# Four input projections of a hybrid mixer as seven products of quarters each

## The chip, the cores and the metric

The kernel runs on one core of a Trainium2 chip. The metric is the device time of one execution in microseconds (us). The engines of the core are TensorE (PE in the profile, its weight loads PEld), VectorE (DVE), ScalarE (ACT), GpSimd (POOL) and SyncE (SP), which issues nearly all DMAs. Each engine takes its own instructions strictly in order and waits at an instruction until the semaphores that it needs have been raised.

## What is computed

One decoder layer on 512 tokens of width 1024, in float32: a SwiGLU feed-forward part, a token mixer and a second feed-forward part, each between two RMS norms.

```python
x = x + 0.5 * rms_norm(swiglu_ffn(rms_norm(x, norm_pre[0]), ffn1_w_in, ffn1_w_out), norm_post[0])
x = x + rms_norm(token_mixer(rms_norm(x, norm_pre[1]), w_mix_in, ...), norm_post[1])
x = x + 0.5 * rms_norm(swiglu_ffn(rms_norm(x, norm_pre[2]), ffn2_w_in, ffn2_w_out), norm_post[2])

def token_mixer(h, w_in, ...):
    hq, hf, hi, hgate, mq, mk, mv, mo, mig, mfg = split_cols(h @ w_in, SPLIT_SIZES)
    # HGRN2 heads from hq, hf, hi, times silu(hgate); mLSTM heads from conv(mq, mk), mv and gates,
    # times sigmoid(mo); both normed, joined, and multiplied by w_out
```

The products `hi`, `hgate`, `mv` and `mo` are each 512 tokens by 1024 inputs by 512 columns.

## The kernel before

A float32 product is made of three TensorE products: each operand is split into a high part (rounded to the type fp32r) and a low part (the rest), and hi·hi, hi·lo and lo·hi are added in PSUM. The normed x of the mixer is held transposed and split in `xq`, four tiles: two halves of the tokens by two halves of the width. Weights come by DMA from SP's queue in tiles of 128 x 1024 values (512 KB) into a ring `raw`; `split` makes the high part on ScalarE (L273) and the low part on VectorE (L275) in one of four slots `w`. `feed` keeps up to four split tiles ahead of TensorE. Where sums of weight tiles are wanted (the feed-forward parts already use seven products for eight), `split` adds them on GpSimd or VectorE (L289).

The mixer writes out its order by hand. Projections are generators in a queue `jobs`; `fill(n)` takes n steps from it, and a step is some 0.7 us of matmuls. The main line calls `fill` between its own small steps, so that TensorE has matmuls while the other engines work on the recurrence. The order of jobs is `hq` (4), `conv` (4), `rows` (the gates), `hi`, `mv`, later `hg` and `mo`. A scheduling layer then orders each engine's instructions by its own model.

The main line is: `forget_gates` (the rest of the `hf` products, sigmoid, log, scans into `G`), on GpSimd meanwhile `gate_weights` and `masks`; then `hgrn_levels` for head pair 0 and for head pair 1. A level takes two differences of `G` on VectorE (L1284, L1285), two exponentials on ScalarE (`qe` L1286, `ke` L1287), a product (L1291), sixteen small matmuls (L1302) and a masked copy (L1306), with `FILL[0]` = 6 or `FILL[1]` = 5 steps of projections between. Then `hgrn_states`, `mlstm_scores`, `mlstm_values`, `hgrn_values` and the output product `mix_out0`, `mix_out1`.

The four projections go through `job_t`: per projection four weight tiles, and for each tile four blocks of 128 tokens by two blocks of 128 inputs by three parts, 96 matmuls of 512 columns in all (L179, L180, L181). ScalarE copies the result of each token block out of PSUM. The residual x stays in the tile `xs` in SBUF from the first feed-forward part until `post1` adds to it (L493).

Of the kernel before, what the change touches and what calls it, by code (L numbers as in the profile page):

```python
# [8 lines left out]
F32 = mybir.dt.float32  # L9
F32R = mybir.dt.float32r  # L10
AF = mybir.ActivationFunctionType
# [3 lines left out]
P = 128  # L15
# [11 lines left out]
QUARTER = 256  # L27
FILL = (6, 5, 2, 2)
NH = 4
# [9 lines left out]


HEAD = 3
FILLED = 4
# [51 lines left out]
FREE2 = (3, 2, 0, 1)  # L94
LIES = {"any": (0, -16, -80, 48), "mix": (-16, 0, -80, 48), "out": (-80, 48, 0, -16)}

# [19 lines left out]
class Layer:  # L116
    def __init__(self, ctx, tc, aps):
        self.tc, self.nc = tc, tc.nc
        self.__dict__.update(aps)
        nc = self.nc  # L120
        pool = lambda name, **kw: ctx.enter_context(tc.tile_pool(name=name, bufs=1, **kw))
        self.cp, self.wp, self.sp, self.psp = pool("cp"), pool("wp"), pool("sp"), pool("psp", space=PSUM)
        self.uid, self.hold = 0, ()
        self.wt, self.free, self.slot = None, deque(), {}

        self.ident = self.cp.tile([P, P], F32, name="ident")
        make_identity(nc, self.ident)
        self.nhalf = self.cp.tile([P, 8], F32, name="nhalf")
        nc.gpsimd.memset(self.nhalf, -0.5)
        self.xs = self.cp.tile([P, NT, D], F32, name="xs")  # L130
# [7 lines left out]
        self.prm = self.cp.tile([P, 36], F32, name="prm")  # L138

    def nm(self, s):  # L140
# [76 lines left out]
    def load_due(self, n):  # L217
        lds = self.due.pop(n, ())
        for ld in lds:
            pool = self.wp if ld.ring == "raw" else self.hpool  # L220
# [29 lines left out]
    def split(self):  # L250
# [5 lines left out]
        if it.dst:  # L256
            w = it.dst()
        else:
            if self.wt is None:
                self.wt = self.wp.tile([P, 2 * D * WBUF + FRONT + PAD], F32R, name="w")  # L260
            if not self.slot and it.key[0] != "mix":
                self.free = deque(FREE2 if it.key[0] == "f2" else FREE)
            n, o = self.lie("out" if it.key[1] == "out" else "mix" if it.key[0] == "mix" and b == 512 else "any")
# [20 lines left out]
        with self.behind(*self.hold):  # L284
            for out, other in it.adds:
                o, c = self.raw[out], self.raw[other]

                late = out[1] >= (HEAD if out[0] == "f1" else 1)
                (nc.vector if late else nc.gpsimd).tensor_tensor(o, o, c, op=ALU.add)  # L289
# [742 lines left out]

    def job_t(self, name, then):

        acc = [self.ps() for _ in range(NT)]
        for k2 in range(ND // 2):
            w = self.pull()
            for i in range(NT):
                for kk in range(2):
                    self.t_mm(acc[i], w, 2 * k2 + kk, kk, i)  # L1040
                    if kk == 0:
                        yield
                if i == NT - 1:
                    self.drop(w)
                if k2 == ND // 2 - 1:
                    then(i, acc[i])
                    if i == NT - 1:
                        self.got.add(name)
                yield

    def mix_items(self):
# [16 lines left out]

        f(HF), f(HQ), f(MQ), t(HI), t(MV), t(HG), t(MO)
        for h in range(2):  # L1070
# [131 lines left out]
    def forget_gates(self, mb):  # L1202
# [14 lines left out]
        for p, f in enumerate(fs):  # L1217
            for a in range(2):
# [3 lines left out]
                )  # L1222
            kk = mb.tile([P, 2, T], F32, tag="kk", bufs=2, name=self.nm("kk"))
            nc.vector.tensor_scalar(kk, f, -1.0, 1.0, op0=ALU.mult, op1=ALU.add)
# [220 lines left out]
    def conv(self, n, ps):  # L1445

        nc = self.nc
        x = self.st("cx")
        nc.scalar.copy(x, ps)
        tap = lambda j: self.prm[:, 4 * j + n : 4 * j + n + 1]  # L1450
        y = self.qk[:, n, :]
# [29 lines left out]
    def mlstm_scores(self, mc):  # L1481
# [14 lines left out]
        nc.scalar.activation(w, w, AF.Exp)  # L1496
        self.qdm = mc.tile([P, 2, 3 * P], F32, name="qdm")
        self.kw = mc.tile([P, 2, 3, P], F32, name="kw")
# [120 lines left out]
    def mixer(self):  # L1619
        nc, tc = self.nc, self.tc  # L1620
        self.got, self.jobs = set(), deque()
        with tc.tile_pool(name="ma", bufs=1) as ma:
# [6 lines left out]
            self.S = self.kdt.rearrange("p h (c v) -> p h c v", v=P)  # L1629
            self.eend = ma.tile([P, 16], F32, name="eend")  # L1630
            with tc.tile_pool(name="mb", bufs=1) as mb:
                self.mb = mb
                kes = [mb.tile([P, 2, T], F32, name=f"ke{n}") for n in range(2)]
                self.q = [mb.tile([P, 2, T], F32, tag="q", bufs=2, name=f"q{p}") for p in range(2)]
# [6 lines left out]
                self.jobs.append(self.job_t("hi", lambda i, ps: nc.scalar.copy(self.vh[:, i].rearrange("p h v -> p (h v)"), ps)))  # L1641
                self.jobs.append(
                    self.job_t("mv", lambda i, ps: nc.scalar.copy(self.vm[:, i, :, :P], ps.rearrange("p (h v) -> p h v", h=NH)))
                )

# [5 lines left out]
                with tc.issue_after(self.pow.ins):  # L1651
                    nc.gpsimd.memset(self.sT, 0.0)
                    self.masks(ma, mb)
                    nc.gpsimd.memset(self.vm[:, :, :, P : P + 1], 1.0)
                self.until("hq3")
                for n in range(NH):
                    nc.scalar.activation(self.q[n // 2][:, n % 2], qps[n], AF.Silu)
                self.hgrn_levels(0, kes, FILL[0])
                self.until("rows")
                nc.scalar.activation(self.qk, self.qk, AF.Silu)  # L1660
                self.hgrn_levels(1, kes, FILL[1], self.gate_rows(ma))
            with tc.tile_pool(name="mc", bufs=1) as mc:
                self.y = mc.tile([P, NT, D], F32, name="y")
                self.jobs.append(self.job_t("hg", lambda i, ps: nc.scalar.activation(self.y[:, i, :W], ps, AF.Silu)))
                self.until("hi")
                self.hgrn_states()
                self.mlstm_scores(mc)
                self.jobs.append(self.job_t("mo", self.gate_mo))
                self.chunks(self.mlstm_values, FILL[2])
# [7 lines left out]
    def gate_mo(self, i, ps):  # L1677
        nc = self.nc
        g = self.st("mo")
        nc.scalar.activation(g, ps, AF.Sigmoid)  # L1680
        y = self.y[:, i, W:]
        nc.vector.tensor_tensor(y, y, g, op=ALU.mult)
# [129 lines left out]
```

## Time and profile before

| | |
|---|---|
| median of 3 runs | 940.24 us (940.08 to 941.1) |
| span of the profiled execution | 938.5 us, 1.74 below the median |
| TensorE busy | 930.2 us, 7471 matmuls |
| VectorE busy | 772.4 us |
| ScalarE busy | 511.9 us |
| GpSimd busy | 107.4 us |

The profile is of one execution. The only time known for the profiled execution itself is its span, from the first instruction to the last; the runs were timed from outside and are other executions. A row of a timeline has the start and the duration in us, the engine, the line of the kernel, the operation and its tiles; what stands in brackets is idle time of the engine just before, and what ended it. A row of a group has the number of instructions, then busy time in us and the mean of one in ns. Durations of neighbours on one engine overlap a little (by about 0.08 us on VectorE).

### The profile page before, as it was taken

To read this page: it belongs to the slowest core of one execution; us is meant where nothing else is said; L and a number is where in the kernel's file an instruction comes from. 1 tells how busy PE (TensorE), PEld (TensorE's weight loads), DVE (VectorE), ACT (ScalarE), POOL (GpSimd) and SP (SyncE) were. 2 spreads that over 40 slices of the span, in tenths; PEclk is the share of its full clock that TensorE was granted. 3 is DMA by queue.
4 is the path that set the end of the run, shared out by engine and by line. 5 is a ranking of instruction groups with operands and counts; after the bars stand their busy time and mean duration, and the time that the engine had idled before them with its cause. 6 is when DMAs were issued, how large, how long until landed. Compare 5 with 4: busy or idle time off the path is not lost.

```text
span 938.5 us, 18056 instructions
## 1 busy us (share of the span) xinstructions
PE 930.2 (99%) x7471; PEld 895.9 (95%) x7471; DVE 772.4 (82%) x1044; ACT 511.9 (55%) x735; POOL 107.4 (11%) x172
## 2 busy tenths in 40 slices
PE   9999999999999999999999999999999999999997
PEld 7999999999999999998887888899999999999997
DVE  6899988889988876698846564799899989998884
ACT  7645555557456467956622444495454545655541
POOL 3530000000001045200001210314000000000101
PEclk9999999999999999999999999999999999999999
DMA  9252433332352024321312124352354434323212
GB/s 319 87 157 91 126 123 113 93 111 72 118 170 90 24 84 124 111 68 45 91 45 68 45 76 139 123 173 65 124 158 135 135 115 156 113 87 121 87 45 90
DMA packets 86956, 101.35 MB, mean 108 GB/s; under 512 B 4277, under 2 KB 66777, under 8 KB 86874
## 3 DMA queue, kind: packets, MB, share of 16 engines
q1 hardware_dynamic: 86586, 99.68, 34.0%
q8 instruction: 58, 0.95, 0.4%
q10 hardware_dynamic: 288, 0.52, 0.2%
q14 instruction: 24, 0.20, 0.1%
HBM read 98.10 MB, written 2.10 MB: 107 GB/s over the span
## 4 chain that ended last, share of the span: by engine, by line
PE 63%; ACT 1%; issue 0%; DVE 0%; DVEq 0%; POOLq 0%; POOL 0%; ACTq 0%
PE ps L603 22%; PE ps L893 7%; PE ps L533 6%; PE ps L901 5%; PE ps L179 5%; PE ps L181 5%; PE ps L180 5%; PE ps L1302 2%; PE ps L543 1%; PE ps L348 1%; PE ps L1476 0%; PE ps L1387 0%; PE ps L1583 0%; PE ps L1556 0%; PE ps L1342 0%; PE ps L1580 0%
## 5 line engine op out<-in xcount | busy, mean ns | idle before, releaser
L273 ACT CAST w<-raw 128x1024 fp32r<-128x1024 f32 (+1 forms) x238 | 244.6, 1035 | 230.3 <-PE ps L603 93.5
L275 DVE TENSOR_TENSOR w<-raw,w 128x1024 fp32r<-128x1024 f32 (+1 forms) x238 | 290.9, 1228 | 36.3 <-ACT w L273 35.8
L603 PE MATMUL ps<-xq,w 128*128 128x256 f32 x2016 | 237.1, 277 | 0.0
L603 PEld LDWEIGHTS ps<-xq,w 128*128 128x128 f32 x2016 | 232.9, 188 | 0.0
L603 PE MATMUL ps<-sq,w 128*128 128x256 f32 x1512 | 177.9, 276 | 0.3
L603 PEld LDWEIGHTS ps<-sq,w 128*128 128x128 f32 x1512 | 174.3, 188 | 0.9 <-ACT ps L654 0.9
L893 PE MATMUL ps<-w,hs 128*128 128x256 f32 x960 | 113.0, 276 | 0.0
L893 PEld LDWEIGHTS ps<-w,hs 128*128 128x128 f32 x960 | 110.7, 188 | 0.0
L289 DVE TENSOR_TENSOR raw<-raw,raw 128x1024 f32<-128x1024 f32 x72 | 89.8, 1251 | 6.1 <-DMA raw<-in_ffn_w_in_dram 4.5
L179 PE MATMUL ps<-w,xq 128*128 128x512 f32 x192 | 78.7, 411 | 0.1
L180 PE MATMUL ps<-w,xq 128*128 128x512 f32 x192 | 74.9, 391 | 0.0
L181 PE MATMUL ps<-w,xq 128*128 128x512 f32 x192 | 74.9, 392 | 0.0
L438 POOL TENSOR_SCALAR col<-col 128x1 f32<-128x1 f32 x24 | 8.9, 372 | 513.7 <-ACT junk L437 513.7
L901 PE MATMUL ps<-w,hs 128*128 128x256 f32 x480 | 57.7, 276 | 0.0
L533 PE MATMUL ps<-xq,w 128*128 128x256 f32 x480 | 56.4, 278 | 0.0
L901 PEld LDWEIGHTS ps<-w,hs 128*128 128x128 f32 x480 | 55.9, 188 | 0.0
L533 PEld LDWEIGHTS ps<-xq,w 128*128 128x128 f32 x480 | 55.2, 188 | 0.5 <-issue 0.5
L179 PEld LDWEIGHTS ps<-w,xq 128*128 128x128 f32 x192 | 36.1, 188 | 8.3 <-issue 0.9
L181 PEld LDWEIGHTS ps<-w,xq 128*128 128x128 f32 x192 | 36.0, 188 | 8.1 <-DVE xq L355 0.3
L812 ACT CAST hs<-hf 128x1024 fp32r<-128x1024 f32 x32 | 33.6, 1052 | 17.6 <-PE ps L901 10.8
L180 PEld LDWEIGHTS ps<-w,xq 128*128 128x128 f32 x192 | 36.2, 188 | 7.0 <-DVE w L281 0.3
L813 DVE TENSOR_TENSOR hs<-hf,hs 128x1024 fp32r<-128x1024 f32 x32 | 39.0, 1219 | 1.3 <-ACT hs L812 1.2
(258 smaller groups left out, 1147.5 us busy)
## 6 DMA issues: line engine op xcount, KB each, us to landing
raw<-in_ffn_w_in_dram SPq DMA_DIRECT2D x98, 512.0 KB, 3.6
raw<-in_ffn_w_out_dram SPq DMA_DIRECT2D x44, 512.0 KB, 3.9
raw<-in_w_mix_in_dram SPq DMA_DIRECT2D x28, 512.0 KB, 3.6
raw<-in_w_mix_out_dram SPq DMA_DIRECT2D x8, 512.0 KB, 3.8
out_dram<-xs SPq DMA_DIRECT2D x8, 256.0 KB, 2.0
xs<-in_x_dram SPq DMA_DIRECT2D x6, 256.0 KB, 4.2
gpost<-in_norm_post_dram SPq DMA_DIRECT2D x3, 512.0 KB, 3.6
gpre<-in_norm_pre_dram SPq DMA_DIRECT2D x2, 512.0 KB, 3.8
```

The costliest lines, as they stand in the source:

```text
L179: mm(ps, sh, mh, start=start, stop=False, **kw)
L180: mm(ps, sh, ml, start=False, stop=False, **kw)
L181: mm(ps, sl, mh, start=False, stop=stop, **kw)
L273: nc.scalar.copy(hi, raw)
L275: self.low = nc.vector.tensor_tensor(lo, raw, hi.bitcast(F32), op=ALU.subtract)
L289: (nc.vector if late else nc.gpsimd).tensor_tensor(o, o, c, op=ALU.add)
L533: mm(ps[:, u0:u1], w[:, a, k, :], self.xop(k, b, u0, u1), start=k + n + m == 0, stop=k == ND - 1 and n == 2, skip_group_check=True,)
L603: self.nc.tensor.matmul(ps[:, c], wb[b][:, k, v], left[d][:, k, :], start=first and a + n + k == 0, stop=n == 2 and k == KH - 1, skip_grou ...
L812: self.nc.scalar.copy(hi, src)
L813: self.nc.vector.tensor_tensor(lo, src, hi.bitcast(F32), op=ALU.subtract)
L893: mm(out, a[kk][:, i * P : (i + 1) * P], w[:, b, kk, QUARTER * v : QUARTER * (v + 1)], start=begin and c == kk == n == 0, stop=kk == 1 and ...
L901: mm(ps[:, QUARTER * c : QUARTER * (c + 1)], A[a][:, c], B[b], start=begin and c == n == 0, stop=n == 2, skip_group_check=True,)
```

## The change

Each of the four projections becomes seven products of quarters (`job_unit`). With x in quarters (tokens by width) and the weights in quarters (width by columns), sums of quarters are formed first, seven products of 256 x 512 by 512 x 256 are made (24 matmuls of 256 columns each), and the four quarters of the result are sums of products. Two of the products add into a bank that holds another one; the others are combined by VectorE, with copies by ScalarE.

- `x_sums` makes four sums of quarters of x, by eight instructions on GpSimd, once for all four projections. They start in the tiles of `vh` and `vm`. Two of them (`p5`, `p7`) are split at once into `xsum`, high part on ScalarE, low part on GpSimd; `p6` (`job_sum`, over `xq[2]`) and `p3` (`last_sum`) are split later, low part on VectorE.
- `xsum` takes the place of `xs` in SBUF: x is written to DRAM (`spill`) at the start of the mixer and read back (`xs2`) before the output product.
- Seven weight tiles are split per projection in place of four; four sums of weight tiles per projection are made on GpSimd. The tiles come in part through the tags `gpre` and `gpost`, whose norm gains are therefore loaded later.
- `FILL[1]` goes from 5 to 4. Some tiles of the mixer move to make room (`early` for `q` and `kk` of pair 0, `qdm`), and the clearing of the last column of `vm` moves behind `last_sum`.

```diff
-FILL = (6, 5, 2, 2)
+FILL = (6, 4, 2, 2)
+UNIT = ("p1", "p5", "p7", "p2", "p6", "p4", "p3")
...
-                late = out[1] >= (HEAD if out[0] == "f1" else 1)
+                late = out[0] != "mix" and out[1] >= (HEAD if out[0] == "f1" else 1)
                 (nc.vector if late else nc.gpsimd).tensor_tensor(o, o, c, op=ALU.add)
...
+    def x_sums(self):
+        nc = self.nc
+        tt = lambda out, a, b, op: nc.gpsimd.tensor_tensor(out, a, b, op=op)
+        kt = lambda v: v.rearrange("p (k t) -> p k t", k=KH)
+        flat = [t.rearrange("p i h v -> p (i h v)") for t in (self.vh, self.vm)]
+        a, b, c, d = (kt(t[:, n : n + D]) for t in flat for n in (0, D))
+        whole = lambda out, q: tt(out, self.xq[q][:, 0].bitcast(F32), self.xq[q][:, 1].bitcast(F32), ALU.add)
+        whole(a, 0)
+        whole(b, 2)
+        tt(c, b, a, ALU.subtract)
+        whole(d, 3)
+        tt(b, b, d, ALU.subtract)
+        tt(a, a, b, ALU.subtract)
+        whole(d, 1)
+        tt(d, d, a, ALU.subtract)
+        self.sums_of = {"p5": b, "p6": a, "p7": c, "p3": d}
+        xs = self.cp.tile([P, 4 * D], F32R, tag="xs", bufs=1, name="xsum")
...
+        self.sum_parts("p5", nc.gpsimd)
+        self.sum_parts("p7", nc.gpsimd)
+
+    def sum_parts(self, p, engine):
+        hi, lo = self.both(self.unit_x[p])
+        self.nc.scalar.copy(hi, self.sums_of[p])
+        engine.tensor_tensor(lo, self.sums_of[p], hi.bitcast(F32), op=ALU.subtract)
...
+    def job_unit(self, name, put, keep):
+        nc, bank = self.nc, {"b6": self.full}
...
+        into = {"p2": "p1", "p4": "p5", "p6": "b6", "p3": "b6"}
+        for p in UNIT:
+            w, x = self.pull(), self.unit_x[p]
+            if p not in into:
+                bank[p] = self.ps()
+            ps, n = bank[into.get(p, p)], 0
+            for a, b in ((0, 0), (0, 1), (1, 0)):
+                for c in range(2):
+                    for k in range(KH):
+                        nc.tensor.matmul(
+                            ps[:, QUARTER * c : QUARTER * (c + 1)], x[:, a, k, P * c : P * (c + 1)], w[:, b, k, :],
+                            start=p not in into and n == 0, stop=(a, k) == (1, KH - 1), skip_group_check=True,
+                        )
+                        n += 1
+                        if n % 6 == 0 and n < 24:
+                            yield
+            self.drop(w)
+            if p == "p1":
+                first = keep(1, 0)
+                nc.scalar.copy(first, two(ps))
+            elif p == "p5":
+                tt(two(bank["b6"]), two(ps), first, ALU.subtract)
+            elif p == "p2":
+                put(0, 0, two(ps))
+            elif p == "p6":
+                rest = keep(1, 1)
+                nc.scalar.copy(rest, two(ps))
+                tt(rest, two(bank["p7"]), rest, ALU.add)
+            elif p == "p4":
+                last = keep(1, 0, two(ps))
+                tt(last, two(ps), rest, ALU.subtract)
...
-        f(HF), f(HQ), f(MQ), t(HI), t(MV), t(HG), t(MO)
+            for p in UNIT:
+                adds = [(key(o), key(i)) for o, i in {"p1": ("ab", "bd"), "p5": ("ad",), "p6": ("ac",)}.get(p, ())]
...
+        f(HF), f(HQ), f(MQ)
+        for u, c0 in enumerate((HI, MV, HG, MO)):
+            unit(u, c0)
...
+            for i in range(NT):
+                nc.sync.dma_start(self.spill[i], self.xs[:, i])
...
                 with tc.issue_after(self.pow.ins):
                     nc.gpsimd.memset(self.sT, 0.0)
                     self.masks(ma, mb)
-                    nc.gpsimd.memset(self.vm[:, :, :, P : P + 1], 1.0)
+                    self.x_sums()
...
                 self.hgrn_levels(0, kes, FILL[0])
+                self.last_sum()
+                nc.gpsimd.memset(self.vm[:, :, :, P : P + 1], 1.0)
...
+                self.xs = self.cp.tile([P, NT, D], F32, tag="xs", bufs=1, name="xs2")
+                for i in range(NT):
+                    nc.sync.dma_start(self.xs[:, i], self.spill[i])
                 self.mix_out0()
```

More of the change, by code (lines that the diff above doesn't have):

```diff
@@ L138, in __init__ @@
         self.prm = self.cp.tile([P, 36], F32, name="prm")
+        dram = ctx.enter_context(tc.tile_pool(name="spill", bufs=1, space=bass.MemoryType.DRAM))
+        self.spill = [dram.tile([P, D], F32, name=f"spill{i}") for i in range(NT)]
     def nm(self, s):
@@ L219, in load_due @@
         for ld in lds:
+            if ld.ring == "gains":
+                tag, n = ("gpre", "gpost")[ld.key[2] == "c"], 1
+                self.raw[ld.key] = self.cp.tile([P, ld.a, ld.b], F32, tag=tag, bufs=n, name=self.nm(tag))
+                continue
             pool = self.wp if ld.ring == "raw" else self.hpool
@@ L262, in split @@
                 self.free = deque(FREE2 if it.key[0] == "f2" else FREE)
-            n, o = self.lie("out" if it.key[1] == "out" else "mix" if it.key[0] == "mix" and b == 512 else "any")
+            kind = "mix" if b >= QUARTER else "any"
+            n, o = self.lie("out" if it.key[1] == "out" else kind if it.key[0] == "mix" else "any")
             self.free.remove(n)
@@ new lines, in job_unit @@
+    def job_unit(self, name, put, keep):
+        nc, bank = self.nc, {"b6": self.full}
+        tt = lambda out, a, b, op: nc.vector.tensor_tensor(out, a, b, op=op)
+        two = lambda t: t.rearrange("p (c f) -> p c f", c=2)
+        into = {"p2": "p1", "p4": "p5", "p6": "b6", "p3": "b6"}
[13 more added lines that the diff above has]
+                        if n % 6 == 0 and n < 24:
+                            yield
+            self.drop(w)
[13 more added lines that the diff above has]
+                tt(last, two(ps), rest, ALU.subtract)
+                put(1, 1, rest)
+                put(1, 0, last)
+            elif p == "p3":
+                put(0, 1, two(ps))
+                self.got.add(name)
+            yield
@@ L1051, in mix_items, with job_kept, put @@
+    def job_kept(self, name, place, func=AF.Copy):
+        def put(u, v, src):
+            if u == 0:
+                self.nc.scalar.activation(place(u, v), src, func)
+            elif v == 0 and func != AF.Copy:
+                for v in range(2):
+                    self.nc.scalar.activation(place(1, v), place(1, v), func)
+        return self.job_unit(name, put, lambda u, v, ps=None: place(u, v))
     def mix_items(self):
@@ L1449, in conv @@
         nc.scalar.copy(x, ps)
+        self.full = ps
         tap = lambda j: self.prm[:, 4 * j + n : 4 * j + n + 1]
@@ L1630, in mixer @@
             self.eend = ma.tile([P, 16], F32, name="eend")
+            self.ma = ma
+            self.early = ma.tile([P, 2, 2, T], F32, tag="first", bufs=1, name="early")
+            for i in range(NT):
+                nc.sync.dma_start(self.spill[i], self.xs[:, i])
             with tc.tile_pool(name="mb", bufs=1) as mb:
@@ L1633, in mixer @@
                 kes = [mb.tile([P, 2, T], F32, name=f"ke{n}") for n in range(2)]
-                self.q = [mb.tile([P, 2, T], F32, tag="q", bufs=2, name=f"q{p}") for p in range(2)]
+                self.q = [self.early[:, 0], mb.tile([P, 2, T], F32, name="q1")]
                 qps = {}
```

64 lines of the change are left out of this document (34 added, 30 removed).

## The prediction

> **What bounds the kernel now.** I read the page's engine totals first, then the chain that ended last, then busy time in windows cut along the mixer, then the order on each engine around the change.
>
> ```profile
> span 938.5 us, 18056 instructions
> ...
> PE 930.2 (99%) x7471; PEld 895.9 (95%) x7471; DVE 772.4 (82%) x1044; ACT 511.9 (55%) x735; POOL 107.4 (11%) x172
> ...
> 355.98 32.64 PE ps L533 x288
> ...
> 403.60 1.73 PE ps L1302 x16
> ...
> 453.75 1.73 PE ps L1302 x16
> ...
> 616.63 68.30 PE ps L603 x600
> ```
>
> TensorE (PE) has work without a gap, and the end chain is one long run of its matmuls. So a matmul removed is time saved, and a wait of TensorE is time lost; nothing later can regain it. The four projections that change begin ahead of the second mark quoted and end with the mixer. TensorE's first and second `hgrn_level` marks (head pair 0 at 403.60, head pair 1 at 453.75) are my milestones below.
>
> ```profile
> 353.00:370.00 17.00, 17.00 (x153) 17.00 (x152) 10.25 (x19) 11.17 (x14) 13.59 (x26) 1.00 0.56 149
> 370.00:388.60 18.60, 18.60 (x167) 18.60 (x166) 12.73 (x21) 18.42 (x19) 5.72 (x10) 1.00 0.35 93
> 388.60:403.60 15.00, 15.00 (x129) 14.52 (x128) 12.27 (x16) 13.59 (x18) 0.00 (x0) 1.00 0.20 63
> 395.40:455.40 60.00, 60.00 (x425) 55.42 (x424) 52.86 (x74) 36.55 (x47) 0.00 (x0) 1.00 0.18 54
> 455.40:481.30 25.90, 25.90 (x157) 22.60 (x156) 14.41 (x23) 10.47 (x16) 0.00 (x0) 1.00 0.28 82
> 481.30:558.30 77.00, 76.95 (x423) 64.56 (x423) 49.24 (x127) 30.29 (x52) 16.18 (x25) 1.00 0.20 62
> ```
>
> After the stretch come the columns PE, PEld, DVE, ACT, POOL. The reserves are thin at two places: ScalarE (ACT) works 18.42 of 18.60 us just ahead of the levels, and VectorE (DVE) 52.86 of 60 inside them. GpSimd (POOL) is empty there, and the change puts its sums into just that gap.
>
> **Fewer products: about 11 us gained.** 384 matmuls of 512 columns (4 projections of 96) become 672 of 256 columns (4 times 7 times 24).
>
> ```profile
> 425.13 0.40 PE L181 MATMUL ps<-w,xq 128*128 128x512 f32 x1
> ...
> 428.58 0.39 PE L181 MATMUL ps<-w,xq 128*128 128x512 f32 x1
> ...
> 542.59 0.39 PE L181 MATMUL ps<-w,xq 128*128 128x512 f32 x1
> ...
> 548.71 0.39 PE L181 MATMUL ps<-w,xq 128*128 128x512 f32 x1
> ```
>
> Fifteen steps lie between the first two starts (0.230 us each), 27 between the last two (0.227). L603 gives 68.30/600 = 0.114 for 256 columns. 384 x 0.2285 = 87.7 us, 672 x 0.114 = 76.6 us: 11 us less, all on the path.
>
> **The wait that it adds on ScalarE: about 19 us lost.** In the changed program's own order, the cast of the first sum of x into `xsum` (`sum_parts`) stands on ScalarE between the first and the second sigmoid of `forget_gates`. It reads the result of GpSimd's fourth sum in `x_sums`, and those stand behind all of `masks`.
>
> ```profile
> 369.67 0.12 POOL L1654 MEMSET vm<- 128x16 f32 x1
> ...
> L289 POOL TENSOR_TENSOR raw<-raw,raw x12: 2392/2408/3446, 23.8 to 647.9; 128x1024 f32<-128x1024 f32 x12
> ...
> 360.98 0.60 ACT L1213 ACTIVATE f<-ps 128x512 f32<-128x512 f32 x1
> 361.48 1.04 ACT L273 CAST w<-raw 128x1024 fp32r<-128x1024 f32 x1
> 362.42 0.60 ACT L1213 ACTIVATE f<-ps 128x512 f32<-128x512 f32 x1
> ...
> 365.62 1.28 ACT L1225 ACT_TABLE_LOAD   x1
> ...
> 398.95 0.61 ACT L1287 ACTIVATE ke<-el 128x512 f32<-128x512 f32 x1
> ```
>
> GpSimd ends its masks at 369.7, and four sums of this size at 2.4 us end at 379.3. ScalarE, free at 361.5, stands until then. Queued behind the cast are the second sigmoid and the cast of the weights of `hq1`: 379.3 + 1.05 + 0.60 + 1.04 = 382.0. TensorE meanwhile has the rest of the forget projections (96 matmuls) and `hq0` (48) from 355.98 at 0.1133 (32.64/288): until 372.3. So it stands 9.7 us, and over 1 us more for the low half of that weight tile, which VectorE makes behind the gate arithmetic.
>
> The wait costs more further on. After the third sigmoid (and one more cast of a sum and of weights) ScalarE runs the chain that began at 365.62 and led to the first `ke` at 398.95 + 0.61 = 399.56, with almost no hole (18.42 of 18.60). It now begins at 382.0 + 1.05 + 0.60 + 1.04 = 384.7, 19.1 later, so that `ke` comes at 418.7. TensorE stood there at 403.60: 15.1 us late, the 11 included. Six more instructions of this size (14 us) follow on GpSimd while VectorE does the forget gates' scans; by the rows of the next part they can hold these back by up to 8 us. Bounds 15 and 23; I take 19.
>
> **More work on VectorE, and GpSimd's sums against it: about 25 us lost.** A projection has 7 weight tiles in place of 4, so 12 more splits in all, besides three combinations of products each and the low parts of two sums of x. Sixteen sums of weight tiles go to GpSimd.
>
> ```profile
> L275 DVE TENSOR_TENSOR w<-raw,w 128x1024 fp32r<-128x1024 f32 (+1 forms) x238 | 290.9, 1228 | 36.3 <-ACT w L273 35.8
> ...
> L622 DVE TENSOR_TENSOR ps<-ps,hf 128x512 f32<-128x512 f32 x37 | 25.7, 695 | 13.5 <-PE ps L603 11.7 <-ACT w L273 1.8
> ...
> 642.12 3.31 POOL L289 TENSOR_TENSOR raw<-raw,raw 128x1024 f32<-128x1024 f32 x1 [3.43 <-DVE w L275]
> 647.86 2.40 POOL L289 TENSOR_TENSOR raw<-raw,raw 128x1024 f32<-128x1024 f32 x1 [2.42 <-DVE w L275]
> ...
> 643.21 3.30 DVE L289 TENSOR_TENSOR raw<-raw,raw 128x1024 f32<-128x1024 f32 x1
> ...
> 647.99 3.36 DVE L275 TENSOR_TENSOR w<-raw,w 128x1024 fp32r<-128x1024 f32 x1 [0.20 <-ACT w L273]
> ...
> 395.44 1.24 DVE L1246 TENSOR_TENSOR kk<-G,kk 128x1024 f32<-128x1024 f32 x1
> ```
>
> A split takes 1.23 us alone. The one that started 0.13 us after a GpSimd sum took 3.36, that is what was left of the sum and then its own time; and GpSimd's sum, when it came second, took 3.31 in place of 2.40. They take turns. [...] By that alone each of the sixteen sums would cost the full 2.4 us wherever VectorE is the limit, and the terms below would come to some 33 us. I take 1.9 per sum, since part of VectorE's instructions here read PSUM or one operand; the bounds are 0 and 2.4.
>
> Between the two milestones' preparations (395.4 to 455.4) VectorE has 52.9 us. By the new order five splits or low parts (5 x 1.23) and three combinations (3 x 0.69) join: 61.1. Seven sums of GpSimd lie there: 7 x 1.9 = 13.3, together 74.4. The start of this work at L1246 now hangs on ScalarE and leads TensorE's mark only by the latency (395.44 to 399.56 = 4.1) where it led by 8.2. So TensorE's second mark comes 70 us after the first, against 50 us of its own work: 20 lost; 6 with nothing blocked, 24 with the full 2.4.
>
> From 455.4 to 481.3 VectorE's 14.4 gets 4 more, in 25.9: covered. From 481.3 to 558.3: 49.2 + 7 x 1.23 + 8 x 0.69 + 8 x 1.9 = 78.5, against 77 less some 4 of matmuls: 5 lost; bounds 0 and 10 (full blocking). Here VectorE also has small chains in which it waits for others, so 5 is no upper end.
>
> **What I cost at nothing.** ScalarE's other additions (12 casts at 1.04, copies of products at about 0.6, like the sigmoid) fit its 36.6 of 60 and 30.3 of 77. The DMAs:
>
> ```profile
> raw<-in_w_mix_in_dram SPq DMA_DIRECT2D x28, 512.0 KB, 3.6
> ...
> 338.32 0.74 DVE L493 SCALAR_TENSOR_TENSOR xs<-hf,col,xs 128x512 f32<-128x512 f32 x1
> ...
> 343.77 0.37 SPq L236 DMA_DIRECT2D raw<-in_w_mix_in_dram  x1
> ...
> 590.45 0.75 DVE L493 SCALAR_TENSOR_TENSOR xs<-y,col,xs 128x512 f32<-128x512 f32 x1 [0.38 <-POOL col L442]
> ```
>
> Four pieces of x of 512 KB leave on SP's queue ahead of the fourth forget weight and the `hq` weights, each some 3.6 us to landing; the third is ready at 339.1, over 4 us before that weight's turn at 343.77, so 0, at most 2 us. They come back behind the last use of `xsum`, over 40 us before their first reader at 590.45; the weights of the output projection queued behind them have two tiles in hand. The two gain rows move there too, with as much room. If SP stood (it waits for GpSimd's last weight sum before one gain row), the output weights would be late by that sum, 2 to 3 us.
>
> **The sum.** -11 + 19 + 20 + 5 = +33 on the span of 938.5: 971.5. The median of the runs is 1.7 above the span; 973. The lower bounds give -11 + 15 + 6 = +10 (950), the upper ones -11 + 23 + 24 + 10 = +46 (986).
>
> **Rivals.** (1) No blocking: GpSimd's sums on the mixer's tiles cost VectorE little, as most of its instructions there are short. ScalarE's wait stays. 950; the doubled durations at 643 and 648 speak against it. 0.20. (2) Faster: GpSimd gets to the sums of x early.
>
> ```profile
> 353.30 0.77 POOL L1373 MEMSET gw<- 128x800 int32 x1 [3.34 <-PE ps L348]
> ...
> 358.93 0.37 POOL L1377 CAST gw<-graw 128x32 fp32r<-128x32 f32 x2 [3.11 <-DMA graw<-in_w_mix_in_dram]
> ```
>
> Its masks took 16.4 us from 353.3, of which 3 were a wait for `graw` and some 4, by my estimate, turns with VectorE; without those the fourth sum ends near 372, `hq1` waits 3 to 4 us and the first level is 8 late; if VectorE then keeps its old lead and blocks little, -11 + 6 + 2 = -3: 937. It decides once all stalls together stay under 11 us. 0.13, as GpSimd would have to be 7 us earlier. Between the two lies no change: 0.04. (3) Worse than all bounds: the small chains of 481 to 558, where `rpow` on GpSimd now queues behind weight sums, add over 10 us: about 995. 0.08. [...]
>
> **Numbers.** The forecast has 0.55, with its own range from 958 to 990. With rival 1 that is 0.75, and the upper end taken to 998 brings in most of rival 3: 944 to 998 leaves out 0.17 to 0.2. Faster by over 0.2% (what a measurement of this kernel can tell) 0.13, within it 0.04, slower 0.83.
>
> **What would show it.** Right: ScalarE idle for over 10 us near 362 to 380 with GpSimd as releaser of an `xsum` cast; TensorE idle ahead of `hq1`, ahead of the first level, and again between the level marks with VectorE as releaser; first level mark near 420, second near 490; splits of over 2 us beside GpSimd's sums; GpSimd busy for about 170 us. Wrong: TensorE without gaps in the mixer, or a second mark before 465. If ScalarE's wait is there but the splits keep 1.2 us, rival 1 holds.

## The result and the profile after

| | before | after |
|---|---|---|
| median | 940.67 us (940.08 to 941.46, 4 runs) | 988.66 us (988.48 to 988.74, 4 runs) |
| span of the profiled execution | 938.5 us | 986.7 us, 2.0 below the median |

The ratio is 1.0511, 95% interval 1.0497 to 1.0524: 48 us slower. The page of the changed kernel, its busy totals, granted clock in 40 slices, and the chain that ended last:

```profile
span 986.7 us, 18728 instructions
...
PE 941.5 (95%) x7759; PEld 920.3 (93%) x7759; DVE 825.7 (84%) x1070; ACT 530.3 (54%) x757; POOL 173.5 (18%) x198
...
PEclk9999999999999997999889998999999999999999
...
PE 43%; DVE 10%; ACT 4%; POOL 4%; issue 3%; DMA 1%; SPq 0%; DVEq 0%; POOLq 0%; ACTq 0%
```

TensorE is idle for 45.2 us where it was for 8.3. Its busy time rose by 11 us although it has less to do, because its clock fell in some slices (51 us at half clock, told below): 18 products of 256 columns (L1099) took 4.21 us there, from 497.96, and 2.39 us at whole clock, from 528.96. VectorE, ScalarE and GpSimd have 10%, 4% and 4% of the end chain, where before TensorE had 63% and no other engine more than 1%. The timeline of four engines about the first level mark, and TensorE's rows at the second mark and the transposes of y (start, duration, engine, line):

```profile
364.80 4.74 POOL L1045 TENSOR_TENSOR vh<-xq 128x1024 f32<-128x1024 f32 x2
...
371.85 2.33 POOL L1045 TENSOR_TENSOR vm<-vh 128x1024 f32<-128x1024 f32 x1
...
374.21 1.04 ACT L1069 CAST xsum<-vm 128x1024 fp32r<-128x1024 f32 x1 [13.13 <-POOL vm L1045]
...
377.27 2.75 DVE L1328 TENSOR_SCALAR early<-f 128x1024 f32<-128x1024 f32 x1
379.94 3.36 DVE L284 TENSOR_TENSOR w<-raw,w 128x1024 fp32r<-128x1024 f32 x1
383.22 2.62 DVE L1393 TENSOR_SCALAR qe<-early 128x512 f32<-128x512 f32 x1
...
383.35 19.29 PE L542 MATMUL ps<-xq,w 128*128 128x256 f32 x140 [5.39 <-DVE w L284]
...
396.21 1.06 ACT L1329 ACTIVATE f<-f 128x1024 f32<-128x1024 f32 x1 [9.30 <-DVE kk L1328]
...
422.72 2.00 PE L1406 MATMUL ps<-qe,ke 128*128 128x64 f32 x16 [1.34 <-ACT ke L1391]
...
490.02 2.08 PE L1099 MATMUL ps<-w,xq 128*128 128x256 f32 x8 [8.24 <-ACT vm L1109]
...
492.17 3.65 PE L1406 MATMUL ps<-qe,ke 128*128 128x64 f32 x16
...
601.24 1.91 PE L357 MATMUL ps<-ident,y 128*128 128x128 f32 x16
```

ScalarE stands 13.1 us for GpSimd's fourth sum, as foreseen; the second sigmoid, behind that cast in its order, starts at 375.17, where it was at 362.42 before. Then comes a second stand of 9.3 us for VectorE, whose instructions take 2.6 to 3.4 us each beside GpSimd's sums. The line numbers are those of the changed kernel: L1406 is the level's matmul, L284 the low part of a split, L1045 a sum of x, L298 a sum of weight tiles, L357 a transpose, L612 a product of the feed-forward parts. The same marks in TensorE's timeline before are at 403.44, 453.59 and 556.42 (the chain that the prediction quotes puts the first two 0.16 later), and its last level stood at 481.12. Busy time by stretch, cut at the marks after (columns as in the prediction):

```profile
355.98:422.70 66.72, 53.11 (x410) 51.65 (x408) 41.26 (x44) 40.27 (x44) 38.22 (x40) 0.87 0.27 70
422.70:492.17 69.47, 56.06 (x437) 54.85 (x437) 67.55 (x75) 41.54 (x52) 22.01 (x8) 0.90 0.12 32
492.17:519.46 27.29, 27.29 (x200) 26.94 (x201) 20.56 (x27) 10.41 (x16) 6.28 (x3) 0.82 0.26 76
519.46:601.24 81.78, 74.05 (x564) 70.80 (x563) 62.23 (x135) 35.97 (x57) 32.67 (x32) 0.94 0.26 83
601.24:646.94 45.70, 43.70 (x203) 34.57 (x201) 25.37 (x37) 21.11 (x43) 5.02 (x14) 1.00 0.51 164
```

To the first mark 19.3 us are lost (47.5 before), between the marks another 19.3 (50.15 before), from there to the last level nothing (27.5 before), then 6.5 to the transposes of y (75.3 before) and 3.1 in the output product (42.6 before). Between the marks VectorE is busy for 67.55 of 69.47 us: that stretch has become VectorE's. TensorE's longest wait there, the 8.2 us up to 490.02, ends with a copy of ScalarE, which had itself stood 4.0 us for VectorE just before.

### The profile page after: what moved, and what is told of

Read it like the earlier page. It is cut to its first block, busy times and chain, and to the rows that moved or that the text cites. A ratio compares the mean times of both kernels' runs of the same rounds, so it can differ in the third digit from the quotient of the medians.

```text
span 986.7 us, 18728 instructions
## 1 busy us (share of the span) xinstructions
PE 941.5 (95%) x7759; PEld 920.3 (93%) x7759; DVE 825.7 (84%) x1070; ACT 530.3 (54%) x757; POOL 173.5 (18%) x198
## 4 chain that ended last, share of the span: by engine, by line
PE 43%; DVE 10%; ACT 4%; POOL 4%; issue 3%; DMA 1%; SPq 0%; DVEq 0%; POOLq 0%; ACTq 0%
PE ps L612 21%; PE ps L902 7%; PE ps L910 5%; PE ps L1099 3%; DVE w L284 2%; PE ps L1406 2%; PE ps L182 1%; PE ps L183 1%; PE ps L184 1%; ACT w L282 1%; DVE qk L1560 1%; POOL col L349 1%; ACT L1767 1%; POOL raw L298 0%; POOL vh L1045 0%
## 5 line engine op out<-in xcount | busy, mean ns | idle before, releaser
L282 ACT CAST w<-raw 128x1024 fp32r<-128x1024 f32 (+1 forms) x242 | 248.6, 1034 | 232.3 <-PE ps L612 89.7
L284 DVE TENSOR_TENSOR w<-raw,w 128x1024 fp32r<-128x1024 f32 (+1 forms) x242 | 302.5, 1256 | 32.7 <-ACT w L282 32.1
L612 PE MATMUL ps<-xq,w 128*128 128x256 f32 x2016 | 237.1, 277 | 0.0
L612 PEld LDWEIGHTS ps<-xq,w 128*128 128x128 f32 x2016 | 232.9, 188 | 0.0
L612 PE MATMUL ps<-sq,w 128*128 128x256 f32 x1512 | 177.9, 276 | 0.3
L612 PEld LDWEIGHTS ps<-sq,w 128*128 128x128 f32 x1512 | 174.3, 188 | 0.9 <-ACT ps L663 0.9
L298 DVE TENSOR_TENSOR raw<-raw,raw 128x1024 f32<-128x1024 f32 x72 | 89.8, 1251 | 6.7 <-DMA raw<-in_ffn_w_in_dram 5.2
L542 PE MATMUL ps<-xq,w 128*128 128x256 f32 x480 | 63.4, 297 | 10.3 <-DVE w L284 5.4
L542 PEld LDWEIGHTS ps<-xq,w 128*128 128x128 f32 x480 | 61.6, 206 | 11.4 <-DVE w L284 5.7
L1099 PE MATMUL ps<-w,xq 128*128 128x256 f32 x384 | 51.7, 288 | 8.2 <-ACT vm L1109 8.2
L1099 PEld LDWEIGHTS ps<-w,xq 128*128 128x128 f32 x384 | 47.5, 191 | 9.5 <-ACT vm L1109 8.4
L298 POOL TENSOR_TENSOR raw<-raw,raw 128x1024 f32<-128x1024 f32 x16 | 43.0, 2691 | 49.1 <-DVE w L284 47.7
L446 ACT ACTIVATE junk<-ps 128x256 f32<-128x256 f32 (+1 forms) x40 | 17.1, 427 | 40.2 <-DVE ps L872 14.1
L910 PE MATMUL ps<-w,xq 128*128 128x256 f32 x288 | 37.2, 276 | 0.0
L631 DVE TENSOR_TENSOR ps<-ps,hf 128x512 f32<-128x512 f32 x37 | 25.7, 696 | 12.5 <-PE ps L612 10.7
```

Of the source, the lines that this page charges most:

```text
L282: nc.scalar.copy(hi, raw)
L284: self.low = nc.vector.tensor_tensor(lo, raw, hi.bitcast(F32), op=ALU.subtract)
L542: mm(ps[:, u0:u1], w[:, a, k, :], self.xop(k, b, u0, u1), start=k + n + m == 0, stop=k == ND - 1 and n == 2, skip_group_check=True,)
L612: self.nc.tensor.matmul(ps[:, c], wb[b][:, k, v], left[d][:, k, :], start=first and a + n + k == 0, stop=n == 2 and k == KH - 1, skip_grou ...
L631: tt = lambda out, a, b, op: nc.vector.tensor_tensor(out, a, b, op=op)
L910: mm(ps[:, QUARTER * c : QUARTER * (c + 1)], A[a][:, c], B[b], start=begin and c == n == 0, stop=n == 2, skip_group_check=True,)
```

## The experiments

The theories, as the expectations name them. Theory 1: GpSimd's sums cost the time, by making ScalarE wait for a result (1a) or by holding VectorE while they run (1b; one expectation calls this the lock). Theory 2: VectorE's own added work is the bound. Theory 3: the half clock behind TensorE's waits is paid in full. Theory 4: TensorE was not the path in the value stages, so fewer products gain nothing. All ratios are to the kernel before, run on the same chip (medians 939.9 to 940.4).

**Weight sums on VectorE.**

```diff
-late = out[0] != "mix" and out[1] >= (HEAD if out[0] == "f1" else 1)
+late = out[0] == "mix" or out[1] >= (HEAD if out[0] == "f1" else 1)
```

> The sixteen sums of weight tiles of the mixer run on VectorE in place of GpSimd; nothing is left out. Theory 1 (GpSimd's sums block VectorE and what waits for them): 16 sums of 2.7 us leave GpSimd and 16 x 1.24 = 20 us come to VectorE without blocking; between the level marks 7 x 1.24 = 9 replace 7 x 2 to 2.4, second mark 3 to 8 earlier relative to the first, time 972 to 985. Theory 2 (VectorE's own work is the bound and blocking is small): 15 to 20 us slower than the changed kernel, 1003 to 1009.

986.44 us, ratio 1.0488 (1.0472 to 1.0504): 2 us better than the change. The marks are at 422.66 and 492.18, as in the changed kernel. Neither theory has its number. Between the marks a weight sum costs the same on either engine, so what it costs there can't be put down to GpSimd's holding VectorE alone. Behind the second mark the engines differ: the transposes of y come at 595.88 in place of 601.24, and 2 of these 5 us are left at the end.

**Weight sums left out.**

```diff
 for out, other in it.adds:
+    if out[0] == "mix":
+        continue
```

> The sixteen sums of weight tiles are left out (products then use single quarters; the loads stay as they are), so that only the sums of x are left on GpSimd. Theory 1: between the level marks 12 to 17 us less than 69.5, the rest of the mixer 5 to 10 less, time 955 to 970, and no VectorE instruction over 2 us after 395. Theory 2: VectorE keeps its 12 more splits and all combinations, time above 980.

971.78 us, ratio 1.0342 (1.0324 to 1.0359): 17 us back, 11.7 of them between the marks (422.74 and 480.47). The sixteen sums are only a third of the loss, a little less than theory 1 asked. VectorE's busy time falls from 825.7 to 806.2, which is 1.2 us for each sum on the mean.

**Matmuls with no use ahead of TensorE's waits.**

```diff
+def warm(self, ps, n):
+    for _ in range(n):
+        self.nc.tensor.matmul(ps[:, :P], self.ident, self.ident, start=True, stop=True)
```

> 180 matmuls of 128 columns with no use (0.11 us each, 20 us) are put on TensorE just ahead of four of its waits, into banks that the next product overwrites: 80 ahead of hq1, 15 ahead of the second diagonal of head pair 0, 40 ahead of its second level, 45 ahead of the first product of mv. They are shorter than the idle times there, so that they should delay nothing, and keep TensorE's clock up. If the half clock behind each wait (periods of 14, 3, 7 and 16 us in the changed kernel) is paid in full (theory 3), the time falls by 12 to 15, to about 975. If in the first three places other chains end last anyway (theory 1), only the period after 490 counts, and the time falls by 3 to 7, to 982 to 986. If the clock is no cause at all: 988 or more.

986.63 us, ratio 1.0493 (1.0477 to 1.0509), span 983.3. The 180 matmuls took 0.227 us each, 41 us in place of the 20 expected: each stands in the trace as two instructions (8119 matmuls against 7759).

```profile
371.37 18.03 PE L182 MATMUL ps<-ident 128*128 128x128 f32 x160
```

The kernel was still 2 us faster. The windows of that kernel:

```profile
355.98:424.20 68.22, 68.22 (x598) 67.74 (x597) 44.45 (x51) 37.16 (x43) 37.75 (x41) 1.00 0.25 66
424.20:490.00 65.80, 65.80 (x573) 65.32 (x572) 57.72 (x63) 34.94 (x42) 20.17 (x8) 1.00 0.12 33
490.00:516.90 26.90, 26.90 (x239) 26.72 (x238) 24.01 (x34) 14.98 (x22) 6.02 (x3) 1.00 0.30 79
```

The clock is whole in these windows (1.00), TensorE never stops, and the marks come at 424.23 and 492.46, no earlier than without. By itself this doesn't clear the clock ahead of the first mark: twice as long as meant, the idle matmuls were on the path there themselves. The first `ke` was ready at 419.35 and waited 4.9 us for TensorE, and ScalarE's order was another as well, with 8 table loads between 362 and that `ke` in place of 12. The changed kernel's own trace says more: ScalarE works from 396.21 to the end of the first `ke` at 422.67 with one hole of 1.25 us, for VectorE, and TensorE stands 1.34 us for that `ke`. So TensorE's clock did not hold the first mark. Behind the second mark no idle matmuls follow; there the last level comes at 516.84 in place of 519.46, and the span is 3 us shorter: this much of the half clock was paid. Theory 3, which asked for 12 to 15, falls as the main cause.

**The parts of the sums of x made later.** A first form moved the two calls in the code only.

```diff
-        self.sum_parts("p5", nc.gpsimd)
-        self.sum_parts("p7", nc.gpsimd)
...
 def job_sum(self):
+    self.sum_parts("p5", self.nc.gpsimd)
+    self.sum_parts("p7", self.nc.gpsimd)
```

> The high and low parts of the first two sums of x (two casts on ScalarE, two subtractions on GpSimd) are made after the gate rows, in place of among the forget gates; nothing is left out. If ScalarE's stand for GpSimd's fourth sum is what makes the first level late (theory 1), the 13.1 us idle ahead of that cast and TensorE's 10.3 us ahead of and in hq1 go, the first level mark comes at 405 to 413 in place of 422.7, and the time is 972 to 980. If VectorE's own load decides (theory 2), the marks and the time stay within 4 us of 988.7, as the work is only moved.

988.25 us, ratio 1.0512 (1.0496 to 1.0529). It tells nothing: the scheduling layer put the casts back between the first two sigmoids, with the same wait of 13.12 us. The second form queues them behind an instruction of ScalarE.

```diff
+    with self.behind(self.rows_made):  # the copy of the gate rows on ScalarE
         self.sum_parts("p5", self.nc.gpsimd)
```

> The high and low parts of three sums of x are queued on ScalarE behind the copy of the gate rows (some 50 us later than in the changed kernel); GpSimd's eight sums of x stay where they are, and nothing is left out. Theory 1a (ScalarE's stand for GpSimd makes the first level late): ScalarE's 13.1 us and TensorE's 10.3 us at hq1 go, first level mark at 403 to 408 in place of 422.7, time 970 to 978. Theory 1b (GpSimd's sums block VectorE wherever they meet it, so the gates' arithmetic on VectorE is now caught by them instead): the stand of ScalarE goes, but gate instructions of 0.55 to 1.25 us take 1.5 to 3.5 in the stretch 362 to 385, first mark at 410 to 418, time 980 to 987.

984.27 us, ratio 1.0462 (1.0446 to 1.0477); first mark 416.69. In its timeline, VectorE's eight scans of the forget gates (2.68 us in all before) and GpSimd's first and last sum of x:

```profile
367.16 21.04 DVE L1338 TENSOR_TENSOR_SCAN G<-one,f 128x128 f32<-128x128 f32 x8 [0.73 <-ACT f L1330]
...
367.38 4.75 POOL L1045 TENSOR_TENSOR vh<-xq 128x1024 f32<-128x1024 f32 x2
...
384.63 2.34 POOL L1045 TENSOR_TENSOR vm<-vm,vh 128x1024 f32<-128x1024 f32 x1
```

ScalarE's stand is gone, and only 6 of the 19.3 us come back: now the scans last as long as GpSimd's sums do, and ScalarE waits 17.9 us for VectorE. Theory 1a falls as the main cause, 1b holds.

**GpSimd's sums of x later as well.**

```diff
+seen = nc.gpsimd.tensor_copy(self.sT[:, 0, :1], self.G[1][:, 1, T - 1 :])
+nc.gpsimd.memset(self.sT[:, 0, :1], 0.0)
+with self.behind(seen):
     self.x_sums()
```

> As the kernel with the parts queued later, and GpSimd's sums of x are queued behind a small copy that reads the last scan of the forget gates, so that they run from about 378 on; nothing is left out. The gates are then undisturbed (ScalarE never idle over 3 us in 360 to 378, hq1 without a wait). Theory 1b: eight sums of 2.4 us now meet the 12 to 14 two-operand instructions of VectorE ahead of the first level, first mark at 408 to 416. Theory 1a: first mark within 3 us of 403.6. Time 970 to 982.

977.65 us, ratio 1.0394 (1.0377 to 1.0412); `hq1` does not wait, the gates are undisturbed, and the first mark is at 410.81, inside the bounds of 1b. The sums now stretch what follows the scans: one product of a level took 4.36 us in place of 0.69, and ScalarE stood 11.93 us for `ek`.

**All sums of x left out, with and without the weight sums.**

```diff
+self.unit_x.update(p5=self.xq[1], p7=self.xq[2], p3=self.xq[3])  # in place of x_sums
```

> All sums of x are left out (the products that need them read plain pieces of x); the sixteen sums of weight tiles stay. Theory 1: first level mark at 403 to 406, time 965 to 972 (19 for the stand and what follows it, and some 3 to 5 for two low parts less on VectorE). Theory 2 (VectorE's other new work is the bound): time above 980.

961.78 us, ratio 1.0225 (1.021 to 1.0241): 26.9 us back, 3 more than theory 1 expected at the most. The first mark is at 402.69, where it was before the change.

> Neither sums of x nor sums of weight tiles: what is left of the change is 672 products of quarters in place of 384 of 512 columns, 12 more splits, the combinations of products, and the way of x through DRAM. If the two groups of sums cost what they cost singly (17 and about 19), the time is 948 to 955. If without them VectorE has room (theory 1 in full), the 11 us of TensorE show and it is 929 to 936. If splits and combinations alone fill VectorE between the levels (theory 2 in part: 58 us between the marks as in the kernel without weight sums, against 50 before), it is 940 to 952.

940.85 us, ratio 1.0009 (1.000 to 1.0019). Both groups together are worth 47.8 us, singly 26.9 and 16.9: they cost a little more together. Everything else in the change comes to nothing, a gain that is eaten. The time lies in the range that was given for theory 2 in part, but not for its reason, which was 58 us between the marks. Its windows, cut at the same marks:

```profile
403.60:453.60 50.00, 49.53 (x425) 48.84 (x423) 46.48 (x65) 29.62 (x38) 0.00 (x0) 1.00 0.15 43
453.60:478.31 24.71, 24.64 (x215) 24.29 (x216) 21.68 (x33) 14.22 (x22) 0.00 (x0) 1.00 0.31 86
478.31:552.40 74.09, 70.01 (x564) 66.79 (x563) 54.69 (x131) 36.01 (x55) 17.04 (x25) 1.00 0.20 58
552.40:601.09 48.69, 45.22 (x202) 35.54 (x201) 27.61 (x41) 21.36 (x43) 5.04 (x14) 0.96 0.51 162
```

The splits and combinations hide: 50.0 us between the marks, as before. The transposes of y start 4.0 us earlier than before (552.40 against 556.42), but the output product takes 6.1 longer (48.69 against 42.63). The timeline of TensorE there, and below it that of the kernel before:

```profile
549.55 3.02 PE L1081 MATMUL ps<-w,xq 128*128 128x256 f32 x24 [2.67 <-ACT mo L1098]
552.40 1.91 PE L359 MATMUL ps<-ident,y 128*128 128x128 f32 x16
557.59 0.50 PE L182 MATMUL ps<-w,xq 128*128 128x512 f32 x1 [3.27 <-ACT xq L365]
```

```profile
556.42 1.91 PE L348 MATMUL ps<-ident,y 128*128 128x128 f32 x16
558.08 0.48 PE L179 MATMUL ps<-w,xq 128*128 128x512 f32 x1
```

The last product of `mo` waits for a copy on ScalarE. Three of the four quarters of its result are multiplied into y only behind that product (VectorE, from 555.70 on), where of four token blocks one was still open when the transposes began (557.36), and the first output matmul starts 5.2 us behind the transposes' start, against 1.7 before. That is 3.5 of the 6.1 us. Another 1.7, half of its 3.4, go to a spell of half clock right behind that wait (558.4 to 561.8; products of 512 columns start 0.43 us apart in it and 0.23 behind it); the rest was not traced.

**Eight GpSimd sums that nobody waits for, in the kernel before.**

```diff
 self.masks(ma, mb)
+for n in range(8):
+    nc.gpsimd.tensor_tensor(v[...], self.xq[n % 4][:, 0].bitcast(F32), self.xq[n % 4][:, 1].bitcast(F32), op=ALU.add)
```

> The kernel before, with eight extra sums on GpSimd behind its masks (128x1024, two operands in SBUF, results that nobody reads, into a tile that is filled only 40 us later). Nobody waits for them. If GpSimd's sums hold VectorE by themselves (theory 1b), instructions of VectorE beside them stretch by up to 2.4 us each (the eight scans of 0.33 us to some 2.7 us each), the first level mark comes 12 to 20 us late and the time is 952 to 962. If only waits for results cost (theory 1a), it stays within 2 us of 940.4.

957.03 us, ratio 1.0179 (1.0153 to 1.0205); first mark 417.88. The eight sums in its timeline:

```profile
370.41 18.72 POOL L1656 TENSOR_TENSOR vh<-xq 128x1024 f32<-128x1024 f32 x8
```

The scans there by their line (shortest, median and longest in ns, first and last start in us):

```profile
L1233 DVE TENSOR_TENSOR_SCAN G<-one,f x8: 387/393/19335, 367.6 to 370.1; 128x128 f32<-128x128 f32 x8
```

Seven of the eight scans took 0.39 us, and not 2.7 each as expected. The eighth, begun at 370.1, took 19.3: it ended with the last sum (389.4 and 389.1). This is theory 1b by itself: 17 us from instructions whose results nobody reads.

**The same with copies, which read one operand.**

```diff
-    nc.gpsimd.tensor_tensor(v[...], ...[:, 0]..., ...[:, 1]..., op=ALU.add)
+    nc.gpsimd.tensor_copy(v[...], self.xq[n % 4][:, 0].bitcast(F32))
```

> The same with eight copies on GpSimd of 128x1024 with one operand, in the place of the sums. If any instruction of GpSimd that reads SBUF holds VectorE for its length, the loss is the copies' time (between 1 and 2.4 us each, by the 1.6 us of a copy of 4x768): 948 to 962. If only two operands against two operands block, it stays within 2 us of 940.4.

945.99 us, ratio 1.0066 (1.0045 to 1.0088). The copies in its timeline take 1.0 us each:

```profile
369.56 7.93 POOL L1656 COPY vh<-xq 128x1024 f32<-128x1024 f32 x8
```

The longest scan lasts 8.5:

```profile
L1233 DVE TENSOR_TENSOR_SCAN G<-one,f x16: 391/400/8523, 367.9 to 385.1; 128x128 f32<-128x128 f32 x16
```

The loss of 6 us is below the 8 to 22 expected, but of the same kind: with one operand on GpSimd's side a scan was held as well, for 8.5 us beside 7.9 us of copies, where it was 19.3 beside 18.7 us of sums.

**48 matmuls left out of the kernel before.**

```diff
-self.t_mm(acc[i], w, 2 * k2 + kk, kk, i)
+self.t_mm(acc[i], w, 2 * k2 + kk, kk, i, 2 * k2 + kk < 3)  # True: two of the three products
```

> The kernel before with 48 of the 384 matmuls of 512 columns left out (the third product of three of eight parts, in each of the four projections), which is 11 us of TensorE: what the change was to take off, and nothing added. If TensorE's work is the path through the mixer (the prediction's first term), the time is 928 to 931. If the chain of small operations of the value stages ends last there anyway (theory 4), the loss of work leaves holes in TensorE and the time is 935 to 940.

930.35 us, ratio 0.9896 (0.988 to 0.9913). The span falls by 10.3 of the 11 us taken out, and the transposes start at 545.80, 10.6 earlier. Theory 4 falls: here matmuls less were time less, as long as nothing was added.

**All sums on VectorE.**

```diff
-nc.gpsimd.tensor_tensor(out, a, b, op=op)
+nc.vector.tensor_tensor(out, a, b, op=op)  # x_sums and its low parts; weight sums as above
```

> All sums on VectorE: those of weight tiles and those of x with their low parts; nothing is left out, and GpSimd has no large work in the mixer. 26 instructions of 1.24 us, 32 us, come to VectorE, and the blocking goes. If the 47 us of the two groups of sums are mostly the lock (each 2.4 us on GpSimd taken from VectorE in full), half of them goes: 960 to 970. If the order of the waits is what costs, it stays at 984 or above.

958.28 us, ratio 1.0192 (1.0171 to 1.0214): 30 of the 48 us are back with the whole computation in place, slightly more than expected. The first mark is at 404.63, 1.2 late, the second at 465.38. It is the best complete version here, and still 18 us behind the kernel before. So theory 2 holds for the sums in part: their load alone costs VectorE 17 us (958.28 against 940.85), while the splits and combinations hide.

## Why the prediction was right, and where it was not

The forecast was 973 us with a range of 944 to 998; 988.66 lies inside, and slower by over 0.2% was right. By its steps:

**Fewer products, -11.** The price is right: 48 matmuls out of the kernel before gave 10.3. That it would all arrive is wrong. Without any sums the change gains nothing (940.85): some 4 us reach the transposes, and the end of `mo` with the half clock behind it takes 6 back. The failing step is "what I cost at nothing": ScalarE's copies and VectorE's combinations were counted as work that fits beside TensorE, and not as what stands between the last product and the output product.

**ScalarE's wait, +19.** The first mark is 19.3 late, and ScalarE, TensorE at hq1 and their releasers are as described. The split is another. GpSimd's masks ended at 364.8 and not 369.7, so ScalarE stood 13.1 us in place of 17.8; what I had as a supplement, GpSimd's further sums holding VectorE, was larger (ScalarE's second stand, 9.3 us, where I had 4 of at most 8). Without ScalarE's stand 13 of the 19 us stay; eight sums without any waiting reader make 14 alone. The size was right because two mechanisms share one time, and the first hid the second; that my two errors cancelled was luck.

**VectorE between the marks, +20.** Measured 19.3; second mark at 492.2 for "near 490". The seven sums there were worth 11.7 by leaving them out, against 7 x 1.9 = 13.3. The rest is 7.6 against 6.7. It goes with the sums of x: without weight sums the stretch is 57.7 us, without either 50.0. It fits the lead that the prediction lost: VectorE's work for the level began 4.1 us ahead of the first mark (418.58), and 8.0 ahead without any sums (395.62). The splits and combinations that were counted in it cost nothing as long as the lead stands. (With nothing blocked the prediction's own figures give 7 and not 6: 61.1 - 4.1 - 50.15.) Rival 1 (no blocking) falls with the scan of 19.3 us. But no run shows the 1.9 a sum, which I had put below 2.4 because part of VectorE's instructions have one operand or read PSUM. Left out, the seven sums gave 1.7 each; on VectorE they cost the stretch as much as on GpSimd (422.66 to 492.18). In the trace a one-operand instruction is held too (L1328, 2.75 us for 0.69); two that read PSUM beside a sum, in the kernel with GpSimd's sums of x later as well, took 1.36 us together (from 399.37), where two without a sum took 1.35 (from 413.02 in the changed kernel).

**Behind the second mark.** Here lies all the missing time. The forecast was 5 lost to the sums against most of the 11 gained, about -6 up to the transposes, and 0 in the output product. Measured: +6.2 and +3.1, together 15.3 more, and the forecast missed by 15.7. From second mark to transposes the kernel without any sums takes 98.8 us (453.60 to 552.40), 4.0 less than before, and the changed kernel 109.1. So the sums cost 10.3 there, where I had 5 (bounds 0 to 10): this term was mis-sized by half. Some 3.7 of the 10.3 are half clock behind TensorE's waits, as with the idle matmuls the stretch took 105.35 us (492.46 to 597.81). The other half of what is missing is the gain that does not arrive. So 988.66 lies above the sum's own upper end (986) and inside the range only because that was stretched for rival 3, which has the place right; whether its reason, small operations of GpSimd queued behind weight sums, took a part was not tried apart.

**The clock.** The prediction has no term for TensorE's clock; it was granted at 1.00 in every stretch that it quotes. After the change it was not. Windows of 4 us about the wait that ends at 490 (the granted clock is the third number from the end):

```profile
484.00:488.00 4.00, 0.00 (x0) 0.00 (x0) 4.00 (x4) 0.09 (x1) 2.80 (x1) 0.63 0.00 0
488.00:492.00 4.00, 1.98 (x8) 1.78 (x8) 4.00 (x7) 4.00 (x6) 0.00 (x0) 0.50 0.12 6
492.00:496.00 4.00, 3.93 (x19) 3.86 (x19) 2.36 (x4) 0.09 (x1) 0.00 (x0) 0.50 0.38 130
```

This spell ends at 502.1. There are six such spells up to 601, 51 us in all. Yet whole clock up to 517 was worth 3 us of span. That the first two stretches are set by other engines was read from the waits; the idle matmuls, themselves in the way ahead of the first mark, don't show it. Behind 517 a spell of 3.4 us (at 593) stood in the kernel with the idle matmuls too; what it costs was not tried apart.

**DMAs, 0.** The way of x through DRAM shows no cost without the sums: none of TensorE's waits in that kernel's mixer ends with a DMA. Whether the late output weights cost something in the changed kernel (one lands on the end chain at 603) was not separated; it can be little, as the output product loses 3.1 us in all and the tail of `mo` takes such an amount alone.

## What to carry to other kernels

Before work is given to an idle GpSimd, look at what VectorE does at that time, and not only at who waits for the result: here eight sums that nobody read cost 17 us, and all the sums of the change cost 17 us on a VectorE that was busy four fifths of the time (958.28 against 940.85), 48 on a GpSimd that was idle. When a wait is taken away, ask what the waiting engine will meet next: ScalarE's stand for GpSimd had sheltered VectorE's scans, and taking it away gave 6 us of 19. A saving on the bounding engine has to be followed to its last consumer; where results that came one by one now come together, the end of the stage pays for it (6.1 us in the output product of the kernel without any sums).

## What the hardware showed that I had not expected

- VectorE and GpSimd don't always take turns. One scan was held for 19.3 us across all eight sums that followed each other without a gap, though by the record it had begun ahead of the first of them (370.1 against 370.41). In the kernel with the parts queued later, where a memset stands between the fourth and the fifth sum, the longest scan was 9.96 us. In the changed kernel splits and gate operations did alternate with the sums (1.45 to 3.44 us each). These runs don't show what decides between the two.
- TensorE's clock changed on a raster of 3.41 us. In the mixer of the changed kernel it fell at 375.8, 406.5, 440.7, 485.0, 570.4 and 594.3; these times lie 9, 10, 13, 25 and 7 steps of 3.41 us apart, and the spells lasted 4, 1, 2, 5, 1 and 2 steps. It fell behind steps in which TensorE had been busy for 0 to 1.45 of the 3.41 us, and not behind one with 1.67 (433.85 to 437.26). With the eight sums that nobody reads it fell at 386.1, behind a step with 0.55 us, and with the idle matmuls at 593.2, behind a step with none. The same wait of 2.3 us, ahead of the first product of sums of x after 565, brought the clock down in the changed kernel (1.11 us busy in that step) and left it whole in the kernel with the idle matmuls (1.92).
- The way back is less plain. The clock was whole again 5.0 us after work came back at 596.1, 6.9 us after 440.6 and 12.1 us after 490.0, each time behind a step with TensorE busy throughout; but three steps with 3.34 to 3.41 us of work (from 440.7, 491.9 and 495.3) did not bring it back.
- A call of a matmul on float32 operands (the idle ones, 128 columns) stands in the trace as two instructions: 360 for 180 calls. Each took 0.113 us (18.03 us for 160), as long as one of 256 columns on the split operands (0.114).
